# Pairs of row tiles of the second product between the gates and ups of the last columns of the first, in a two-layer encoder

## The chip, the cores and the metric

The kernel runs on one core of a Trainium2 chip. The metric is the device time of one execution in microseconds (us); several runs were timed, and their median counts. The engines have these names: PE (TensorE, matmuls), DVE (VectorE), ACT (ScalarE), POOL (GpSimd), SP (SyncE, which issues the loads).

## The reference

Two layers over x of 256 tokens by 1024, float32. Each layer has an FFN, a mixer of two attention groups, and an FFN, with a LayerNorm behind each. The change touches the four FFNs alone. D_FF is 2816.

```python
def swiglu(x, w_in, w_out):
    h = x @ w_in
    gate, up = h[..., :D_FF], h[..., D_FF:]
    return (jax.nn.silu(gate) * up) @ w_out
...
for l in range(DEPTH):
    x = layer_norm(ALPHA * x + 0.5 * swiglu(x, ffn1_w_in[l], ffn1_w_out[l]), ln_g[l, 0], ln_b[l, 0])
    mix = hybrid_mixer(x, cos, sin, mask, w_in[l], w_out[l], diff_lambda[l],
                       diff_subln_g[l], swa_sink[l], lambda_init)
    x = layer_norm(ALPHA * x + mix, ln_g[l, 1], ln_b[l, 1])
    x = layer_norm(ALPHA * x + 0.5 * swiglu(x, ffn2_w_in[l], ffn2_w_out[l]), ln_g[l, 2], ln_b[l, 2])
```

## The kernel before

**Halves.** Every float32 operand is split in two parts, a high one (wh, gh) and the low rest (wl, gl), and a product is the sum of three matmuls: wh with gh, wl with gh, wh with gl. A row of weights (128 x 1024) comes by a DMA of 512 KB into `raw`; ACT casts it to wh (L118), DVE subtracts to get wl (L119). `Weights.get` makes rows ahead of their use, up to LOOK + 1 = 9 tiles of wh and wl; a pair (below) counts as four. Five `raw` buffers take the loads, and a pair uses three of them.

**One FFN** (named by layer and number: 00, 02, 10, 12) is made of these stages, in this order on PE, whose order is the order of the code. The other engines' instructions are set into order by a scheduler with priorities; the making of weights (`LATER`) comes behind other work that is ready.

- `first`: column tiles 0 to 3 of the first product (of 22, JT), from 8 rows of weights, and their transposes.
- `col` for columns 4 and 5 alone, then for two columns at once: (6, 7) to (20, 21). A column has a gate half and an up half, each with one PSUM bank: 8 wide matmuls (wh against both parts of x, 512 columns, L419) and 8 narrow ones (wl against the high part, 256 columns, L424). Two columns take four of the eight PSUM banks; the next two take the other four. Once a half is done, ACT copies its narrow part out (L434), and DVE adds the two parts (L435), which frees the bank. Then come silu, the product (L438) and the split into g (L441, L442).
- The second product. Its 22 row tiles belong to the columns of the same number. A single (`step`) multiplies one row tile for both token tiles and both halves of the width: 12 matmuls of 512 columns. Two row tiles together can be a pair (`pair`), after Strassen and Winograd: seven products in place of eight, 21 matmuls for 24. For this DVE makes four sums of the weights (L86 to L89) and the split of all of them, and `sums` makes four sums of g (L457 to L462). Pairs are those of columns (6, 7) to (16, 17), STR = 3 to 8. `PLAN` sets singles and pairs behind one another: three singles, six pairs. Four banks (acc) take the output, four more (pp: products 5, 7, 1, 6) what the outputs have in common.
- Behind the last pair the pp are added into x on DVE (L541 to L550), and a tail of TAIL = 7 singles goes over token tile 0, then over token tile 1, so that the LayerNorm of tile 0 runs beside the matmuls of tile 1. The transposes for the next stage follow.

Of the kernel before, what the change touches and what calls it, by code (L numbers as in the profile page):

```python
# [19 lines left out]
P = 128  # L20
# [13 lines left out]
TAIL = 7  # L34
SPLIT = 3
TCUT = 3
LOOK = 8
# [3 lines left out]
STR = (3, 4, 5, 6, 7, 8)  # L41
PLAN = "o o S o S S S S S"
# [17 lines left out]
class Weights:  # L60
# [6 lines left out]
    def _halves(self, i, raw, nm=""):  # L67
        nc = self.nc
        n = raw.shape[-1]
        wh = self.pool.tile([P, 1024], F32R, tag="wh", name=f"wh{i}{nm}", bufs=9)  # L70
        wl = self.pool.tile([P, 1024], F32R, tag="wl", name=f"wl{i}{nm}", bufs=9)
        nc.scalar.copy(wh[:, 0:n], raw)
        nc.vector.tensor_tensor(wl[:, 0:n], raw, wh[:, 0:n].bitcast(F32), ALU.subtract)
        return [tuple(w[:, c : c + 512] for w in (wh, wl)) for c in range(0, n, 512)]
# [21 lines left out]
    def _slots(self, i):  # L96
        return 4 if self.srcs[i][0] == "S" else 1

    def _make(self, i):
        nc = self.nc  # L100
        if self.srcs[i][0] == "S":
            return self._make_pair(i)
        raw = self.pool.tile([P, 1024], F32, tag="raw", name=f"raw{i}", bufs=5)
        wh = self.pool.tile([P, 1024], F32R, tag="wh", name=f"wh{i}", bufs=9)
        wl = self.pool.tile([P, 1024], F32R, tag="wl", name=f"wl{i}", bufs=9)

        n = 512 if i < 3 else 1024
        src = self.srcs[i]

        rows = src if isinstance(src, tuple) else (src,)  # L110
        for c in range(0, 1024, n):
            s = slice(c, c + n)
            for q, r in enumerate(rows):
                h = P // len(rows)

                (nc.sync if i or c else nc.scalar).dma_start(raw[q * h : (q + 1) * h, s], r[:, s])
            with self.tc.high_priority(0 if i < 3 else -LATER):
                nc.scalar.copy(wh[:, s], raw[:, s])  # L118
                nc.vector.tensor_tensor(wl[:, s], raw[:, s], wh[:, s].bitcast(F32), ALU.subtract)  # L119
        self.made.append((wh, wl))  # L120
# [15 lines left out]
def encoder_kernel(  # L136
# [36 lines left out]

    singles = [k for k in range(JT) if k // 2 not in STR]
    singles, tail = singles[: len(singles) - TAIL], singles[len(singles) - TAIL :]
    plan, left, pairs = [], list(singles), list(STR)
    for u in PLAN.split():
        plan.append((u, (left if u == "o" else pairs).pop(0)))
    assert not left and not pairs

    def out_rows(w):
        row = lambda k: w[k * P : (k + 1) * P, :]
        rows = [row(k) if u == "o" else ("S", row(2 * k), row(2 * k + 1)) for u, k in plan]
        return rows + [row(k) for k in tail]

    srcs = []
    for l in range(DEPTH):
        srcs += [f1_b[l, k] for k in range(KT)]
        srcs += [f1_in[l, j, s] for j in range(JT - NB) for s in range(2)]
        srcs += out_rows(f1_out[l])  # L190
# [8 lines left out]
        srcs += [f2_b[l, k] for k in range(KT)]  # L199
        srcs += [f2_in[l, j, s] for j in range(JT - NB) for s in range(2)]  # L200
        srcs += out_rows(f2_out[l])
# [159 lines left out]
    def ffn(l, n, last=False):  # L361
        nonlocal wi
        nm = f"{l}{n}"
        gs = [gp.tile([P, 2, 2, SEQ], F32R, tag="g", name=f"g_{nm}_{q}") for q in range(JT // 2)]
# [29 lines left out]
        def first_t(gv, t):  # L394
            tr = ps.tile([P, 4, P], F32, tag="b", name=f"trg_{nm}{t}")
            for i in range(4):
                nc.tensor.transpose(tr[:, i, :], gv[:, i * P : (i + 1) * P], ident)
            for q in range(2):
                a = slice(t * P, (t + 1) * P)
                dh = gs[q][:, :, 0, a]  # L400
                nc.scalar.copy(dh, tr[:, 2 * q : 2 * q + 2, :])
                dv.tensor_tensor(gs[q][:, :, 1, a], tr[:, 2 * q : 2 * q + 2, :], dh.bitcast(F32), ALU.subtract)

        def col(*js, flip=False):
# [3 lines left out]
            for j in js:  # L408

                hs = [ps.tile([P, 2, SEQ], F32, tag="b", name=f"h{'gu'[s]}_{nm}_{j}") for s in range(2)]  # L410
                tl = tp.tile([P, 2, SEQ], F32, tag="tl", name=f"tl_{nm}_{j}", bufs=2)
# [3 lines left out]

            def wide(hs, ws, s):
                for k in range(KT):

                    mm(hs[s], ws[s][0][:, k * P : (k + 1) * P], xx[:, k], start=(k == 0 and not flip),  # L419
                       stop=(k == KT - 1 and flip), skip_group_check=flip)  # L420

            def narrow(hs, ws, s):
                for k in range(KT):
                    mm(hs[s][:, 1, :], ws[s][1][:, k * P : (k + 1) * P], xx[:, k, 0], start=(k == 0 and flip),  # L424
                       stop=(k == KT - 1 and not flip), skip_group_check=flip)

            one, two = (narrow, wide) if flip else (wide, narrow)
            for j, hs, tl, ws in ts:
                for s in range(2):
                    one(hs, ws, s)  # L430
            for j, hs, tl, ws in ts:
                for s in range(2):
                    two(hs, ws, s)
                    nc.scalar.copy(tl[:, s], hs[s][:, 1, :])  # L434
                    dv.tensor_tensor(tl[:, s], hs[s][:, 0, :], tl[:, s], ALU.add)  # L435
                nc.scalar.activation(tl[:, 0], tl[:, 0], AF.Silu)  # L436
                gv = tl[:, 1]
                dv.tensor_tensor(gv, tl[:, 0], gv, ALU.mult)  # L438
                q, jj = divmod(j, 2)
                n = P if q in STR and jj == 0 else SEQ  # L440
                nc.scalar.copy(gs[q][:, jj, 0, 0:n], gv[:, 0:n])  # L441
                dv.tensor_tensor(gs[q][:, jj, 1, 0:n], gv[:, 0:n], gs[q][:, jj, 0, 0:n].bitcast(F32), ALU.subtract)  # L442
                if q in STR and jj:
                    sums(q, ts[0][2][:, 1], gv)

        sm = {}
# [31 lines left out]
        for j in (NB + 1, *range(NB + 2, JT, 2)):  # L478

            col(*((j,) if j == NB + 1 else (j, j + 1)), flip=(j % 4 == 0 or j == NB + 1))  # L480
# [8 lines left out]
        k0, k1 = singles[0], tail[-1]  # L489
        kl = tail[-SPLIT]  # L490
        acc = [[(slice(512 * h, 512 * h + 512), ps.tile([P, 512], F32, tag="b", name=f"acc_{nm}_{t}{h}"),
                 k0, tail[-SPLIT - 1] if last and t and h else k1) for h in range(2)] for t in range(2)]
# [12 lines left out]
        pp = {}  # L505

        def pair(q, w, first, final):
            b11, b21, b22, t4, t1, t2, t3 = w
            if first:
                for c in (5, 7, 1, 6):  # L510
                    pp[c] = ps.tile([P, 512], F32, tag="b", name=f"pp_{nm}_{c}")
            sh, sl = sm[q]
            blk = lambda kk, t: [gs[q][:, kk, e, t * P : (t + 1) * P] for e in range(2)]
            smb = lambda c: (sh[:, c], sl[:, c])
            s1, s2, s3, s4 = (smb(c) for c in range(4))
            for o, (ah, al), (bh, bl) in (
                (acc[0][0][1], blk(1, 0), b21),
                (acc[0][1][1], s4, b22),
                (pp[5], s1, t1),
                (pp[7], s3, t3),  # L520
                (pp[1], blk(0, 0), b11),
                (pp[6], s2, t2),
                (acc[1][0][1], blk(1, 1), t4),
            ):
                own = any(o is p for p in pp.values())
                for e, (g, ww) in enumerate(((ah, bh), (ah, bl), (al, bh))):
                    mm(o, g, ww, start=(own and first and e == 0), stop=(own and final and e == 2))  # L527

        for u, k in plan:
            w = W.get(wi)  # L530
            wi += 1
            if u == "S":
                pair(k, w, k == STR[0], k == STR[-1])
            else:
                for t in range(2):
                    step(k, w, t, acc[t])
        v = tp.tile([P, 512], F32, tag="tmp", name=f"v_{nm}")
        c = 0.5 / ALPHA
        lo, hi = slice(0, 512), slice(512, 1024)
# [17 lines left out]
        if last:  # L557

            fin = [acc[1][0]] + [(slice(o, o + 256), ps.tile([P, 256], F32, tag="b", name=f"acc_{nm}_1{o}"),
                                  kl, k1) for o in (512, 768)]  # L560
# [421 lines left out]
```

## Time and profile before

| what | value |
|---|---|
| median of 3 runs | 930.16 us |
| lowest, highest | 928.87, 930.35 us |
| profiled execution, its own time | 929.28 us |
| its span, first to last instruction | 927.5 us |
| mean granted clock of PE | 0.997 |
| DMA, mean over the span | 190 GB/s |

The page of the profile gives busy time and share of the span for each engine. In rows of a group stands the line, the engine, the operation, what it writes and reads (out<-in) with the shapes, the count, the busy time with the mean of one in ns, and the idle time of the engine just before them with what ended it. In rows of the timeline stands the start, the duration, then the same names, and in brackets the idle time ahead, where there was any. A row with x8 is eight instructions in a run. In a view by windows each stretch has a row. Matmuls are pipelined: a row of eight ends later than the next begins, and a matmul's cost is the distance between starts.

### The profile page before, as it was taken

How to read it: one execution, taken by the hardware profiler on the slowest of the kernel's cores; microseconds unless marked ns; L12 is line 12 of the kernel's file. 1: busy time of each engine (PE TensorE's matmuls, PEld its weight loads, DVE VectorE, ACT ScalarE, POOL GpSimd, SP SyncE). 2: the span in 40 equal slices, each digit the busy share in tenths (PEclk: the TensorE clock that was granted, in tenths of full speed). 3: DMA queues.
4: the chain of work that ended last, by engine and by line, in shares of the span. 5: the costliest groups of instructions: out<-in, count | busy, mean ns of one | idle time of the engine just before them, and what ended most of it. 6: DMA issues, size and time to landing. Idle time of an engine off the chain costs nothing.

```text
span 927.5 us, 13795 instructions
## 1 busy us (share of the span) xinstructions
PE 919.1 (99%) x4958; PEld 784.9 (85%) x4958; DVE 804.9 (87%) x1388; ACT 577.8 (62%) x982; POOL 17.0 (2%) x27
## 2 busy tenths in 40 slices
PE   9999999999999999999999999999999999999996
PEld 6888888888878888888888888888888888888885
DVE  7898899998987677899986888999988876888997
ACT  5768656546865666656646666664478656666660
POOL 0000000000000000000000000000000000000000
PEclk9999999999999999999999999999999999999998
DMA  8976445774426755545775665466844365665451
GB/s 320 313 265 203 160 137 191 246 260 154 128 90 206 248 182 182 159 136 191 257 262 196 187 192 168 136 231 208 290 112 137 100 236 188 189 192 163 136 205 46
DMA packets 51380, 176.30 MB, mean 190 GB/s; under 512 B 6512, under 2 KB 8304, under 8 KB 51312
## 3 DMA queue, kind: packets, MB, share of 16 engines
q1 hardware_dynamic: 51024, 175.03, 58.0%
q8 instruction: 39, 0.64, 0.3%
q10 hardware_dynamic: 288, 0.39, 0.1%
q14 instruction: 29, 0.24, 0.1%
HBM read 174.35 MB, written 1.05 MB: 189 GB/s over the span
## 4 chain that ended last, share of the span: by engine, by line
PE 98%; DMA 1%; DVE 1%; SPq 0%; issue 0%; ACT 0%; DVEq 0%
PE hg L419 14%; PE hu L419 14%; PE acc L503 12%; PE hb L381 9%; PE hu L424 7%; PE hg L424 7%; PE pp L527 7%; PE acc L527 5%; PE ao L840 5%; PE os L776 1%; PE pj_sq L617 1%; PE pj_sq L619 1%; PE pj_dv L617 1%; PE pj_sq L618 1%; PE pj_dq L618 1%; PE pj_dv L619 1%
## 5 line engine op out<-in xcount | busy, mean ns | idle before, releaser
L119 DVE TENSOR_TENSOR wl<-raw,wh 128x1024 fp32r<-128x1024 f32 (+1 forms) x271 | 325.2, 1207 | 57.0 <-PE hg L424 20.2
L118 ACT CAST wh<-raw 128x1024 fp32r<-128x1024 f32 (+1 forms) x271 | 282.1, 1046 | 99.7 <-PE acc L503 14.8
L419 PE MATMUL hg<-xx,wh 128*128 128x512 f32 x576 | 143.1, 390 | 0.0
L419 PE MATMUL hu<-xx,wh 128*128 128x512 f32 x576 | 142.3, 389 | 0.0
L419 PEld LDWEIGHTS hu<-xx,wh 128*128 128x128 f32 x576 | 108.1, 188 | 22.5
L419 PEld LDWEIGHTS hg<-xx,wh 128*128 128x128 f32 x576 | 106.6, 188 | 21.2
L503 PE MATMUL acc<-wh,g 128*128 128x512 f32 (+1 forms) x326 | 90.5, 386 | 0.0
L424 PE MATMUL hg<-xx,wl 128*128 128x256 f32 x576 | 81.0, 283 | 0.0
L424 PE MATMUL hu<-xx,wl 128*128 128x256 f32 x576 | 80.9, 283 | 0.0
L424 PEld LDWEIGHTS hg<-xx,wl 128*128 128x128 f32 x576 | 75.4, 191 | 1.6
L424 PEld LDWEIGHTS hu<-xx,wl 128*128 128x128 f32 x576 | 74.3, 192 | 0.0
L503 PEld LDWEIGHTS acc<-wh,g 128*128 128x128 f32 x326 | 60.9, 188 | 12.2
L381 PE MATMUL hb<-wh,xx 128*128 128x512 f32 x256 | 69.5, 391 | 0.4 <-ACT wh L118 0.4
L381 PEld LDWEIGHTS hb<-wh,xx 128*128 128x128 f32 x256 | 47.7, 188 | 11.3 <-ACT wh L118 1.6
L503 PE MATMUL acc<-wl,g 128*128 128x512 f32 (+1 forms) x163 | 51.7, 385 | 0.0
L434 ACT COPY tl<-hg 128x256 f32<-128x256 f32 x72 | 26.7, 371 | 30.9 <-PE hg L419 27.4
L434 ACT COPY tl<-hu 128x256 f32<-128x256 f32 x72 | 26.9, 373 | 19.6 <-PE hu L424 16.8
L381 PE MATMUL hb<-wl,xx 128*128 128x512 f32 x128 | 38.9, 390 | 0.0
L441 ACT CAST g<-tl 128x128 fp32r<-128x128 f32 (+1 forms) x72 | 26.7, 371 | 19.2 <-DVE tl L438 18.2
L840 PE MATMUL ao<-wh,xx 128*128 128x512 f32 x128 | 37.0, 398 | 0.0
L503 PEld LDWEIGHTS acc<-wl,g 128*128 128x128 f32 x163 | 30.6, 188 | 6.1
L436 ACT ACTIVATE tl<-tl 128x256 f32<-128x256 f32 x72 | 30.1, 418 | 6.5 <-DVE tl L435 5.7
(1140 smaller groups left out, 1576.3 us busy)
## 6 DMA issues: line engine op xcount, KB each, us to landing
raw<-in_f_in_dram SPq DMA_DIRECT2D x144, 512.0 KB, 4.4
raw<-in_f_out_dram SPq DMA_DIRECT2D x40, 512.0 KB, 4.5
raw<-in_m_in_dram SPq DMA_DIRECT2D x36, 512.0 KB, 4.4
raw<-in_f_b_dram SPq DMA_DIRECT2D x29, 512.0 KB, 4.3
raw<-in_m_out_dram SPq DMA_DIRECT2D x8, 512.0 KB, 5.0
raw<-in_m_out_dram SPq DMA_DIRECT2D x16, 256.0 KB, 4.4
lng<-in_ln_g_dram SPq DMA_DIRECT2D x6, 512.0 KB, 4.9
lnb<-in_ln_b_dram SPq DMA_DIRECT2D x6, 512.0 KB, 6.2
```

What stands on the lines that cost most here:

```text
L118: nc.scalar.copy(wh[:, s], raw[:, s])
L119: nc.vector.tensor_tensor(wl[:, s], raw[:, s], wh[:, s].bitcast(F32), ALU.subtract)
L381: mm(hb[s], xx[:, k, g, t, :], ww[:, 512 * s : 512 * s + 512], start=(k == 0 and e == 0), stop=(k == KT - 1 and e == 2))
L419: mm(hs[s], ws[s][0][:, k * P : (k + 1) * P], xx[:, k], start=(k == 0 and not flip), stop=(k == KT - 1 and flip), skip_group_check=flip)
L424: mm(hs[s][:, 1, :], ws[s][1][:, k * P : (k + 1) * P], xx[:, k, 0], start=(k == 0 and flip), stop=(k == KT - 1 and not flip), skip_group_c ...
L434: nc.scalar.copy(tl[:, s], hs[s][:, 1, :])
L436: nc.scalar.activation(tl[:, 0], tl[:, 0], AF.Silu)
L441: nc.scalar.copy(gs[q][:, jj, 0, 0:n], gv[:, 0:n])
L503: mm(a, g, ww[:, s], start=(k == ka and e == 0), stop=(k == kb and e == 2))
L527: mm(o, g, ww, start=(own and first and e == 0), stop=(own and final and e == 2))
L617: mm(o, xx[:, k, 0, t, :], wh[:, s], start=(k == 0), stop=False)
L840: mm(acc[t][h], xx[:, k, g, t, :], ww[:, s], start=(k == 0 and e == 0), stop=(k == KT - 1 and e == 2))
```

## The change

- There are seven pairs in each FFN, those of columns (4, 5) to (16, 17), STR = 2 to 8. No single stands ahead of the pairs any more, and the tail has eight.
- The pairs stand among the columns. From column MIX = 14 on, columns come one by one: three products of a pair (9 matmuls), the gate half, the other four products (12 matmuls), the up half. Column 20 has the seventh pair, column 21 none.
- All seven products of the pairs have a bank of their own from column 14 to 20 (pp 1 to 7; products 2, 3 and 4 go on as the acc banks in the tail), so that the gate and up halves of these columns share the one bank that is left. The fourth acc bank is taken after column 21.
- LOOK is 7 for 8: eight tiles of wh and wl of 1024 columns; the halves of 512 columns of a pair have two tiles of their own, and a pair counts as three.
- The high and low parts of the sums of pairs 5 to 8 are in the pool of g, and tiles of g are taken when they are written first.

```diff
-TAIL = 7
+TAIL = 8
-LOOK = 8
+LOOK = 7
-STR = (3, 4, 5, 6, 7, 8)
-PLAN = "o o S o S S S S S"
+STR = (2, 3, 4, 5, 6, 7, 8)
+MIX = 14
...
     def _halves(self, i, raw, nm=""):
...
-        wh = self.pool.tile([P, 1024], F32R, tag="wh", name=f"wh{i}{nm}", bufs=9)
-        wl = self.pool.tile([P, 1024], F32R, tag="wl", name=f"wl{i}{nm}", bufs=9)
+        tag, bufs = ("", LOOK + 1) if n == 1024 else ("f", 2)
+        wh = self.pool.tile([P, n], F32R, tag="wh" + tag, name=f"wh{i}{nm}", bufs=bufs)
+        wl = self.pool.tile([P, n], F32R, tag="wl" + tag, name=f"wl{i}{nm}", bufs=bufs)
...
-        return 4 if self.srcs[i][0] == "S" else 1
+        return 3 if self.srcs[i][0] == "S" else 1
...
+        def half(j, s, tl):
+            nonlocal wi
+            h, w = bank(j, s), W.get(wi)
+            wi += 1
+            wide(h, w)
+            narrow(h, w)
+            gather(h, tl, s)
...
-            if STR.index(q) < 3:
-                s = xp.tile([P, 2, 4, P], F32R, tag="x", name=f"s_{nm}_{q}")
-                sh, sl = s[:, 0], s[:, 1]
-            else:
-                sh, sl = (tp.tile([P, 4, P], F32R, tag="tmp", name=f"s{c}_{nm}_{q}") for c in "hl")
+            pool, tag = (xp, "x") if STR.index(q) < 3 else (gp, "g")
+            s = pool.tile([P, 2, 4, P], F32R, tag=tag, name=f"s_{nm}_{q}")
+            sh, sl = s[:, 0], s[:, 1]
...
-        for j in (NB + 1, *range(NB + 2, JT, 2)):
+        for j in (NB + 1, *range(NB + 2, MIX, 2)):
...
+        def pair(i, w):
+
+            b11, b21, b22, t4, t1, t2, t3 = w
+            q = STR[i]
...
+            todo = ((2, blk(1, 0), b21), (3, s4, b22), (5, s1, t1), (7, s3, t3),
+                    (1, blk(0, 0), b11), (6, s2, t2), (4, blk(1, 1), t4))
+            for m, (c, (ah, al), (bh, bl)) in enumerate(todo):
+                if c not in pp:
+                    pp[c] = ps.tile([P, 512], F32, tag="b", name=f"pp_{nm}_{c}")
+                if m == 3:
+                    yield
+                for e, (g, ww) in enumerate(((ah, bh), (ah, bl), (al, bh))):
+                    mm(pp[c], g, ww, start=(i == 0 and e == 0), stop=(c in (1, 5, 6, 7) and i == len(STR) - 1 and e == 2))
+            yield
+
+        for j in range(MIX, JT):
+            tl = tl_tile(j)
+            if j - MIX < len(STR):
+                w = W.get(wi)
+                wi += 1
+                run = pair(j - MIX, w)
+            for s in range(2):
+                if j - MIX < len(STR):
+                    next(run)
+                half(j, s, tl)
+            gated(j, tl)
+            loads(j)
+
...
+        c22 = ps.tile([P, 512], F32, tag="b", name=f"acc_{nm}_11")
+        acc = [[(lo, pp[2], None, tail[-1]), (hi, pp[3], None, tail[-1])],
+               [(lo, pp[4], None, tail[-1]), (hi, c22, tail[0], tail[-SPLIT - 1] if last else tail[-1])]]
```

`gather` is the copy and the add (L434, L435 before; L418, L419 after), `gated` is silu, product and split, both as they were.

The order of PE at column 14 of FFN 00, before: the wide matmuls of columns 14 and 15 in four banks (hg and hu are gate and up, xx is the transposed x), then the narrow ones.

```order
L419 MATMUL hg_00_14_999<-xx_78,wh28_766 128x512 x8
L419 MATMUL hu_00_14_1000<-xx_78,wh29_772 128x512 x8
L419 MATMUL hg_00_15_1014<-xx_78,wh30_781 128x512 x8
L419 MATMUL hu_00_15_1015<-xx_78,wh31_787 128x512 x8
L424 MATMUL hg_00_14_999<-xx_78,wl28_767 128x256 x8
L424 MATMUL hu_00_14_1000<-xx_78,wl29_773 128x256 x8
L424 MATMUL hg_00_15_1014<-xx_78,wl30_782 128x256 x8
L424 MATMUL hu_00_15_1015<-xx_78,wl31_788 128x256 x8
```

The same place now, from the last matmuls of a pair's first three products (pp is a product, s a sum of g) to the second group:

```order
L531 MATMUL pp_00_5_1027<-wl28t_785,s_00_2_470 128x512
L531 MATMUL pp_00_5_1027<-wh28t_784,s_00_2_470 128x512
L409 MATMUL hg_00_14_1032<-xx_78,wh29_889 128x512 x8
L414 MATMUL hg_00_14_1032<-xx_78,wl29_890 128x256 x8
L531 MATMUL pp_00_7_1031<-wh28t_784,s_00_2_470 128x512
L531 MATMUL pp_00_7_1031<-wl28t_785,s_00_2_470 128x512
```

Each half now stands alone, wide and narrow together, with a part of a pair on each side; nine matmuls of products 1, 6 and 4 and then the up half follow.

The order of DVE in FFN 02, now, behind the add of the up half of column 17: the making of a pair's weights (raw128, wl128, t4), the gating of column 17 (L424, L430), the sums of g for pair 8 (sf, s; L476 to L481), and in the last row the add of the gate half of column 18.

```order
L89 TENSOR_TENSOR raw128a_4356<-raw128b_4357,raw128t_4358 128x512
L424 TENSOR_TENSOR tl_02_17_4245<-tl_02_17_4245 128x256
L74 TENSOR_TENSOR wl128b_4367<-raw128b_4357,wh128b_4366 128x1024
L476 TENSOR_TENSOR sf_02_8_4347<-tl_02_16_4138,tl_02_17_4245 128x128
L430 TENSOR_TENSOR g_02_8_4238<-tl_02_17_4245,g_02_8_4238 128x256
L477 TENSOR_TENSOR sf_02_8_4347<-tl_02_16_4138,sf_02_8_4347 128x128
L90 TENSOR_TENSOR t4_128_4361<-raw128b_4357,raw128a_4356 128x512
L479 TENSOR_TENSOR sf_02_8_4347<-tl_02_17_4245,sf_02_8_4347 128x128
L74 TENSOR_TENSOR wl128t_4371<-raw128t_4358,wh128t_4370 128x1024
L74 TENSOR_TENSOR wl128a_4375<-raw128a_4356,wh128a_4374 128x1024
L481 TENSOR_TENSOR s_02_8_4348<-sf_02_8_4347,s_02_8_4348 128x512
L419 TENSOR_TENSOR tl_02_18_4355<-hg_02_18_4391,tl_02_18_4355 128x256
```

Before, most of the making of pairs' weights stood behind the adds of all columns; now it stands between them.

The order of DVE in FFN 00, now, at the last columns: from the add of gate 20 over rows of weights to the adds of the products 1, 6 and 5 (L566 to L571) and the add of up 20 among them.

```order
L419 TENSOR_TENSOR tl_00_20_1652<-hg_00_20_1668,tl_00_20_1652 128x256
L120 TENSOR_TENSOR wl51_1655<-raw51_1653,wh51_1654 128x1024
L120 TENSOR_TENSOR wl52_1671<-raw52_1669,wh52_1670 128x1024
L566 SCALAR_TENSOR_TENSOR x_in0_596<-pp_00_1_1066,x_in0_596 128x512
L569 TENSOR_TENSOR v_00_1803<-pp_00_6_1070,v_00_1803 128x512
L120 TENSOR_TENSOR wl53_1677<-raw53_1675,wh53_1676 128x1024
L419 TENSOR_TENSOR tl_00_20_1652<-hu_00_20_1717,tl_00_20_1652 128x256
L571 TENSOR_TENSOR u_00_1807<-pp_00_5_1027,v_00_1803 128x512
```

The adds of the products stood behind all columns and pairs (L541 to L550); they now start before the columns end.

More of the change, by code (lines that the diff above doesn't have):

```diff
@@ L171, in encoder_kernel, with ffn_rows @@
     dv = nc.vector
[L174 to L183, printed above, removed]
+    tail = [k for k in range(JT) if k // 2 not in STR]
+    assert len(tail) == TAIL and len(STR) <= JT - MIX
+    def ffn_rows(b, w_in, w_out):
+        row = lambda k: w_out[k * P : (k + 1) * P, :]
+        rows = [b[k] for k in range(KT)]
+        for j in range(NB, JT):
+            if j >= MIX and j - MIX < len(STR):
+                q = STR[j - MIX]
+                rows.append(("S", row(2 * q), row(2 * q + 1)))
+            rows += [w_in[j - NB, 0], w_in[j - NB, 1]]
         return rows + [row(k) for k in tail]
@@ L408, in col @@
             for j in js:
-                hs = [ps.tile([P, 2, SEQ], F32, tag="b", name=f"h{'gu'[s]}_{nm}_{j}") for s in range(2)]
-                tl = tp.tile([P, 2, SEQ], F32, tag="tl", name=f"tl_{nm}_{j}", bufs=2)
+                hs = [bank(j, s) for s in range(2)]
+                tl = tl_tile(j)
                 ws = [W.get(wi), W.get(wi + 1)]
@@ L414, in col @@
                 ts.append((j, hs, tl, ws))
[L416 to L425, printed above, removed]
             one, two = (narrow, wide) if flip else (wide, narrow)
@@ L477, in ffn, with loads @@
         first_t(g1, 1)
[L478 to L480 removed]
+        def loads(j):
+            nonlocal gb
             if first_x and j == NB + 2:
```

113 lines of the change are left out of this document (53 added, 60 removed).

## The prediction, made before the changed kernel had run

> **What bounds the kernel now.** I read the page first: busy times, the granted clock in slices, and the chain that ended last.
>
> ```profile
> PE 919.1 (99%) x4958; PEld 784.9 (85%) x4958; DVE 804.9 (87%) x1388; ACT 577.8 (62%) x982; POOL 17.0 (2%) x27
> PEclk9999999999999999999999999999999999999998
> PE 98%; DMA 1%; DVE 1%; SPq 0%; issue 0%; ACT 0%; DVEq 0%
> ```
>
> TensorE (PE) works for 99% of the span at nearly the full clock, and it is 98% of the chain. A matmul less is a matmul of time less, as long as nothing else makes PE wait. VectorE (DVE) at 87% is the engine to watch. So I cut one FFN (layer 0, second: "02") at its stages: columns 4 to 13, columns 14 to 21, the singles and pairs, the last seven rows.
>
> ```profile
> core 0: us, PE busy (x) PEld busy (x) DVE busy (x) ACT busy (x) POOL busy (x), PEclk, DMA share, GB/s
> 305.80:361.90 56.10, 56.10 (x328) 49.75 (x327) 41.92 (x78) 35.95 (x66) 0.00 (x0) 1.00 0.63 197
> 361.90:406.30 44.40, 44.40 (x258) 39.37 (x256) 38.48 (x73) 28.71 (x52) 0.00 (x0) 1.00 0.51 156
> 406.30:443.00 36.70, 36.70 (x163) 30.41 (x162) 35.44 (x43) 23.04 (x27) 0.00 (x0) 1.00 0.56 186
> 443.00:462.80 19.80, 19.80 (x93) 16.46 (x92) 19.80 (x29) 11.57 (x13) 0.92 (x1) 1.00 0.71 245
> ```
>
> PE is full in every stage. VectorE's load is uneven: 87% in columns 14 to 21, 97% in the pairs. It never stops PE there, because columns have four PSUM banks and their results wait, and because halves of the weights are made rows ahead. The change moves pairs among columns and takes three of the four banks away. That is where the time is decided.
>
> **What goes: twelve matmuls.** Two row tiles as singles are 24 matmuls of 512 columns (3 products, 2 token tiles, 2 halves of the width, twice); as a pair they are 21. Each FFN makes a seventh pair, so 3 matmuls go per FFN, 12 in all.
>
> ```profile
> 133.52 0.39 PE L527 MATMUL acc<-wh46b,g 128*128 128x512 f32 x1
> ...
> 138.28 0.61 PE L503 MATMUL acc<-wh,g 128*128 128x512 f32 x2
> ```
>
> Between these lie the 21 matmuls of one pair: 4.76 us, 0.227 each (the duration of 0.39 is latency; start to start counts). 12 x 0.227 = **2.72 us** saved at most: 929.28 - 2.72 = 926.56. The profiled execution (929.28) lies 0.88 below the median of the runs shown, 930.16, and within their spread; I keep to it.
>
> **What PE does in the mixed stretch.** A half column (gate or up) is 8 wide and 8 narrow matmuls.
>
> ```profile
> 394.22 1.12 PE L424 MATMUL hu<-xx,wl 128*128 128x256 f32 x8
> 395.18 1.12 PE L424 MATMUL hg<-xx,wl 128*128 128x256 f32 x8
> ...
> 400.86 1.98 PE L419 MATMUL hu<-xx,wh 128*128 128x512 f32 x8
> 402.67 1.98 PE L419 MATMUL hg<-xx,wh 128*128 128x512 f32 x8
> ```
>
> 0.96 + 1.81 = 2.77 us. The order of the mixed stretch is 9 matmuls of a pair (2.04), gate (2.77), 12 matmuls (2.72), up (2.77): a unit of 10.3 us. No instruction is dearer there than in the stretches it came from.
>
> **The wait that is added.** All halves of columns 14 to 20 use one bank. A half may start once the half before it has been gathered: ScalarE copies the narrow part, VectorE adds (L434, L435; L418, L419 after). Up's start is covered by 12 matmuls behind the gate (2.72 us), the next gate's by 9 (2.04). PE is in order: what waits at the head of a half holds the pair's matmuls behind it too, and ready ones among them cannot pass. So the **lag** counts, from a half's last matmul to the end of its add.
>
> ```profile
> 315.66 0.84 PE L419 MATMUL hu<-xx,wh 128*128 128x512 f32 x3
> ...
> 316.26 0.42 DVE L435 TENSOR_TENSOR tl<-hg,tl 128x256 f32<-128x256 f32 x1 [1.19 <-ACT tl L434]
> 395.94 0.41 DVE L435 TENSOR_TENSOR tl<-hg,tl 128x256 f32<-128x256 f32 x1
> 396.27 0.41 DVE L435 TENSOR_TENSOR tl<-hu,tl 128x256 f32<-128x256 f32 x1
> ```
>
> With VectorE idle (it waited 1.19) the lag is 316.68 - 315.66 = 1.02 (the gate ended where up began). With a full queue, the gate of column 19, which ended where the up at 394.22 began, was added by 395.94 + 0.41 = 396.35: 2.13. In the middle, 1.58. All lie under 2.72, and 2.13 just misses 2.04: in the mean the bank is covered, and what costs is where VectorE has much to do ahead of an add.
>
> **What VectorE must do per stretch.** I price its instructions start to start in a full queue.
>
> ```profile
> 137.43 0.69 DVE L86 TENSOR_TENSOR raw50t<-raw50a 128x512 f32<-128x512 f32 x1
> ...
> 144.10 1.22 DVE L73 TENSOR_TENSOR wl50t<-raw50t,wh50t 128x1024 fp32r<-128x1024 f32 x1
> 145.24 1.22 DVE L73 TENSOR_TENSOR wl50a<-raw50a,wh50a 128x1024 fp32r<-128x1024 f32 x1
> ...
> 148.18 1.22 DVE L73 TENSOR_TENSOR wl51b<-raw51b,wh51b 128x1024 fp32r<-128x1024 f32 x1
> 149.31 0.68 DVE L88 TENSOR_TENSOR raw51a<-raw51b,raw51t 128x512 f32<-128x512 f32 x1
> 149.91 1.22 DVE L73 TENSOR_TENSOR wl51t<-raw51t,wh51t 128x1024 fp32r<-128x1024 f32 x1
> ...
> 159.87 1.23 DVE L119 TENSOR_TENSOR wl<-raw,wh 128x1024 fp32r<-128x1024 f32 x1
> ...
> 388.17 0.28 DVE L457 TENSOR_TENSOR sf<-tl,tl 128x128 f32<-128x128 f32 x1
> 388.37 0.68 DVE L87 TENSOR_TENSOR raw132t<-raw132a,raw132b 128x512 f32<-128x512 f32 x1
> ```
>
> 1024 elements: 1.135 (1.14 and 1.13); 512: 0.60; 256: 0.33 (the two adds above); 128: 0.20. Together they fall a little short: from 137.43 to 159.87 stand 11 of 1024 and 16 of 512, by these 22.09, measured 22.44, 1.6% more.
>
> In the changed order, from the add of gate 14 to that of gate 20 in FFN 02, VectorE has 30 instructions of 1024, 29 of 512, 22 of 256 and 10 of 128: 34.05 + 17.4 + 7.26 + 2.0 = 60.7, with the 1.6% 61.7. PE has six units, 61.8. **The two are level**: a burst is caught up only slowly. The worst burst is the piece of VectorE's order shown with the change (FFN 02; 10 and 12 have the same): behind the add of up 17, twelve instructions up to the add of gate 18, three of 1024, three of 512, three of 256, three of 128: 3.405 + 1.8 + 0.99 + 0.6 = 6.80, with 1.6% 6.90. PE needs 2.04 + 2.77 = 4.81 from one half's end to the other's. The lag grows by 2.09: from 1.58 to 3.67, and the cover is 2.72. Up 18 starts **0.95 us late**. Then the queue is short (five instructions to the next add, against 5.49 of PE), and the next long piece (to gate 19: 6.22, with 1.6% 6.32, against 4.81) ends at a lag of 1.02 + 1.51 = 2.53, still covered by 2.72. Worked through in this way, FFN 00, whose order differs, loses 0.15 once.
>
> So 3 x 0.95 + 0.15 = 3.0. From below: with the lag of 1.02 ahead of the burst 3 x 0.39 = 1.2. From above, with 2.13: 3 x 1.5 + 0.15 = 4.6. I take the middle. To it comes ScalarE, which stands ahead of each add with its copy.
>
> ```profile
> L118 ACT CAST wh<-raw 128x1024 fp32r<-128x1024 f32 x265 | 278.3, 1056 | 94.6 <-PE acc L503 14.8 <-PE hg L419 11.9 <-PE hu L419 10.1
> 402.87 0.37 ACT L434 COPY tl<-hu 128x256 f32<-128x256 f32 x1 [0.20 <-PE hu L419]
> ```
>
> Here the copy met an idle engine. But a cast of 1.06 us is under way in 278.3/927.5 = 30% of the time, and met in its middle it delays the copy by 0.53: 0.16 a copy. Six halves are near their limit (gates 18 and 19 in three FFNs): 1.0 us; bounds 0 and 6 x 1.06 = 6.4. Stalls in all: **4.0 us**.
>
> **What else moves, at nothing.** The halves of a pair's weights are made among the columns rather than in a block; the instructions are the same but for one more pair per FFN, 44 more on VectorE in the whole program, all priced above or hidden under a full PE in the tail. The look-ahead is one row shorter (eight tiles for nine); between pairs PE takes 2.77 us a row, and a load lands in 4.4 to 4.5:
>
> ```profile
> raw<-in_f_in_dram SPq DMA_DIRECT2D x144, 512.0 KB, 4.4
> raw<-in_f_out_dram SPq DMA_DIRECT2D x40, 512.0 KB, 4.5
> ```
>
> A unit loads four rows of 0.52 MB, 2.1 MB in 10.3 us, 204 GB/s; the last stage above moved 245 beside a full PE, so SyncE's queue keeps up. If it doesn't, the price is a late cast, which is the ScalarE term. The tail has 8 rows for 7: 12 matmuls moved, none new, and they give the LayerNorm 1.36 us more cover. Column 21 has no pair ahead of it, but its gate and up take the banks of products 1 and 6, not the shared one: on VectorE's order the adds from those banks (L566, L569) stand ahead of the add of up 20, some 5 us before they are needed.
>
> **The sum:** 929.28 - 2.72 + 4.0 = **930.6 us**.
>
> **The rivals.**
>
> (a) *All adds come in time.* Speaks for it: VectorE's sum is just under PE's, and lags of 1.02 were seen. Against: the burst of 6.9 against 4.81 needs a lag under 0.63 ahead of it. No stall: 929.28 - 2.72 = **926.6**.
>
> (b) *VectorE becomes the bound of the mixed stretch: slower.* Its place is columns 14 to 20, its price each microsecond over PE's 61.8 in an FFN, and it decides from 2% over my prices (60.7 x 1.02 = 61.9). At 5% over, 63.7 against 61.8, 1.9 an FFN and the bursts beside it: row by row 2.7 in 02, 10 and 12, 1.6 in 00, 9.6 in all, **936.2**. For it: 1.6% of the 2 is in the trace already, and every wait of VectorE on a cast counts. Against: where VectorE was at 97%, it did not slip.
>
> (c) *Column 21 does wait for the one bank*, or the banks of 1 and 6 come as late as that: two adds without cover in each FFN, 8 x 1.02 = 8.2 and no other stall: 926.56 + 8.16 = **934.7**. Against it speaks the order of VectorE.
>
> (d) *The clock drops in the mixed stretch*, because PE now stops and starts there.
>
> ```profile
> 0.77 3.92 PE L217 MATMUL wps<-const-bfloat16-1.0 128*128 128x512 bf16 x9 [0.77 <-PEq L971]
> ```
>
> After idling, nine matmuls of 512 columns took 3.92 us, 0.436 each, against 0.227: 1.9 us lost. Once per FFN 7.5: 930.6 + 7.5 = **938.1**. Against: the granted clock was 1.00 in all four stages above, and my stops are about 1 us, an idling far shorter than a start from nothing. The Trainium skill, "TensorE: Matmul & The Clock Gate", section "A second HAM failure mode: psum-queue depth-cycling", tells of a kernel in which PSUM banks cycled and PE paused so often that the clock swung between half and full; the same page puts the idle gap that loses the clock at some 3 us. By the first the time would be that of (d), by the second that of the forecast, and no row of before shows pauses of this kind.
>
> **How the numbers follow.** About 0.2% (1.86 us) is what a measurement of this kernel can tell from no change: faster means stalls under 0.86, slower over 4.6. Chances: forecast 0.56, with a range of its own from 1.2 to 5.6 of stalls (4.6 and the 1.0), 927.8 to 932.2; (a) 0.17; (b) 0.19; (c) 0.04; (d) 0.04. Of the forecast's 0.56 I put 0.04 below and 0.07 above the band. Faster: 0.17 + 0.04 = 0.21. Slower: 0.19 + 0.04 + 0.04 + 0.07 = 0.34. Same: 0.45. The range runs from (a), 926.5, to (b) at 5%, 936.2; outside it lie (d), (b) beyond 5%, and half of (a)'s scatter, together under 0.2.
>
> **What the profile after would show.** Right: PE's matmul count 12 lower; idle time on PE ahead of L409 hu of column 18 in FFNs 02, 10 and 12, near 1 us, released by VectorE's add in L419, and little elsewhere; VectorE near 98% busy from column 14 to 20; no idle time at column 21; clock 1.00. Idle time at most halves of columns 14 to 20 would speak for (b), at column 21 for (c), a clock under 0.95 for (d). The forecast is wrong if PE waits on casts of weights or loads at the head of a pair (the look-ahead too short), or if idle time stands where I count none: at the banks of column 14 or ahead of the tail.

## The result and the profile after

| | median | runs |
|---|---|---|
| before | 929.88 us | 4, 928.87 to 930.35 |
| changed | 936.1 us | 4, 934.96 to 938.29 |
| ratio | 1.0071 | 95% interval 1.0051 to 1.0092 |

The changed kernel is slower by 0.7%, 6.2 us. The profiled execution took 935.84 us with a span of 933.4, 5.9 more than before. Its page has these lines on the engines, the clock and the chain:

```profile
PE 919.9 (99%) x4946; PEld 781.4 (84%) x4946; DVE 821.1 (88%) x1432; ACT 571.3 (61%) x991; POOL 17.0 (2%) x27
PEclk9999999999999999999999999999999999999999
PE 31%; DVE 3%; DMA 1%; ACT 1%; issue 1%; DVEq 0%; ACTq 0%; SPq 0%
```

The twelve matmuls are gone (4946 for 4958) and the clock is full. But the chain no longer runs on PE from end to end: steps on VectorE, ScalarE and loads stand in it. The same stages of FFN 02 as before, by windows; first columns 4 to 13, then the mixed stretch, columns 14 to 20:

```profile
core 0: us, PE busy (x) PEld busy (x) DVE busy (x) ACT busy (x) POOL busy (x), PEclk, DMA share, GB/s
306.60:362.70 56.10, 56.10 (x327) 49.78 (x326) 46.94 (x90) 36.57 (x68) 0.00 (x0) 1.00 0.53 177
362.70:437.00 74.30, 72.33 (x367) 61.16 (x366) 71.61 (x108) 49.65 (x74) 0.00 (x0) 1.00 0.65 206
```

In the mixed stretch PE lacks 2.0 us, VectorE is busy for 96%, and the loads run at 206 GB/s, for 156 in columns 14 to 21 before. The view of PE's waits names what it waits for, with the total, the times and the longest:

```profile
PE hu L409 <- DVE tl L419: 3.2, 5, 1.0
PE hg L409 <- DVE tl L419: 2.4, 3, 1.2
```

All eight waits stand at the head of a half in the mixed stretch, and all end with VectorE's add, as foreseen. This view counts from a matmul's modelled end. Taken from start to start of the matmuls, over the usual 0.227, the eight add to 6.9 us (0.60 and 0.92 in FFN 00, 0.98 and 1.31 in 02, 1.17 and 0.39 in 10, 1.16 and 0.33 in 12). The first matmul behind each wait takes 0.11 more.

One of the eight is the burst that the prediction worked out. From VectorE's timeline, the add of up 17 and what stands behind it; the second row of PE's is the half that waits:

```profile
405.33 0.42 DVE L419 TENSOR_TENSOR tl<-hu,tl 128x256 f32<-128x256 f32 x1 [0.21 <-ACT tl L418]
405.68 0.68 DVE L89 TENSOR_TENSOR raw128a<-raw128b,raw128t 128x512 f32<-128x512 f32 x1
...
411.56 0.69 DVE L481 TENSOR_TENSOR s<-sf,s 128x512 fp32r<-128x512 f32 x1
412.17 0.42 DVE L419 TENSOR_TENSOR tl<-hg,tl 128x256 f32<-128x256 f32 x1
```

```profile
411.44 0.39 PE L531 MATMUL pp<-wh125f,g 128*128 128x512 f32 x1
412.64 1.20 PE L409 MATMUL hu<-xx,wh 128*128 128x512 f32 x4 [0.81 <-DVE tl L419]
```

From add to add 6.84 us (6.90 forecast); up 18 starts 412.64 - 411.44 - 0.227 = 0.97 late (0.95 forecast). The same half waits in FFNs 10 and 12.

Other waits begin elsewhere. In FFN 00, ahead of gate 15, a row of VectorE's making of the pair before, then the rows of SyncE, ScalarE, VectorE and PE:

```profile
88.69 1.22 DVE L74 TENSOR_TENSOR wl31t<-raw31t,wh31t 128x1024 fp32r<-128x1024 f32 x1
```

```profile
89.97 0.33 SPq L83 DMA_DIRECT2D raw34b<-in_f_out_dram  x1
```

```profile
94.64 1.05 ACT L73 CAST wh34b<-raw34b 128x1024 fp32r<-128x1024 f32 x1 [3.35 <-DMA raw34b<-in_f_out_dram]
95.60 0.36 ACT L418 COPY tl<-hu 128x256 f32<-128x256 f32 x1
```

```profile
95.99 0.42 DVE L419 TENSOR_TENSOR tl<-hu,tl 128x256 f32<-128x256 f32 x1 [0.55 <-ACT tl L418]
```

```profile
96.47 1.20 PE L409 MATMUL hg<-xx,wh 128*128 128x512 f32 x4 [0.44 <-DVE tl L419]
```

Up 14 was done at 93.80, where the next pair's matmuls begin. Its copy is due then, but ahead of it in ScalarE's order stands the cast of a pair's second row, and that row, issued at 89.97, has not landed. It was issued right behind VectorE's last reading of raw31t, a buffer of the pair before (88.69 + 1.22 = 89.91). ScalarE is idle for 3.35 us, the last 0.84 of them with the copy ready behind the cast, and then the cast itself takes its time. Copy, add and the next half come late one after the other: up 14's copy starts 1.80 after its matmuls, where 0.20 was seen before. The Trainium skill, "TensorE: Matmul & The Clock Gate", section "Architectural detail: the array is 16× 32×32, not 1× 128×128", calls ScalarE and VectorE strict first-in-first-out queues; these rows agree.

A late load stands ahead of the other seven waits too, in most of them less directly. Ahead of the burst at up 18 in FFN 02 it holds the copy of up 17, with whose add the burst begins:

```profile
403.98 1.05 ACT L73 CAST wh128b<-raw128b 128x1024 fp32r<-128x1024 f32 x1 [3.38 <-DMA raw128b<-in_f_out_dram]
404.94 0.36 ACT L418 COPY tl<-hu 128x256 f32<-128x256 f32 x1
```

So the burst begins with a lag of 1.7 us in FFN 02 and, by the like rows, of 1.9 in FFNs 10 and 12, where 1.58 was forecast. Ahead of up 19 in FFNs 10 and 12 the copy of up 18 is held in the same way, by a cast that is idle for 2.4. Ahead of gate 19 in FFN 00 VectorE is idle for 0.88 until ScalarE has cast a tile of g, which stood behind a pair's cast idle for 2.02. At gate 20 in FFN 02, the longest wait, the copy of up 19 stands behind the cast of a single row:

```profile
427.44 1.05 ACT L119 CAST wh<-raw 128x1024 fp32r<-128x1024 f32 x1 [2.60 <-PE pp L531]
```

The view puts this idle time down to PE, but the row's load was issued at 421.69 and landed at 427.36, just before the cast began.

Twenty casts of pairs wait for their load in this kernel, 41.9 us in all; in the kernel before it is one, for 0.4. The longest of them before and after, and what SyncE waits for most ahead of a pair's loads (the last sum of the pair before, which frees a buffer), by the views of the waits:

```profile
ACT wh46b L72 <- DMA raw46b<-in_f_out_dram: 0.4, 1, 0.4
```

```profile
ACT wh46b L73 <- DMA raw46b<-in_f_out_dram: 3.8, 1, 3.8
```

```profile
SPq L83 <- DVE t L90: 61.5, 15, 6.3
```

### The profile page after: what moved, and what is told of

It is laid out like the page before. It is cut to its first block, busy times and chain, and to the rows that moved or that the text cites. A ratio compares the mean times of both kernels' runs of the same rounds, so it can differ in the third digit from the quotient of the medians.

```text
span 933.4 us, 13768 instructions
## 1 busy us (share of the span) xinstructions
PE 919.9 (99%) x4946; PEld 781.4 (84%) x4946; DVE 821.1 (88%) x1432; ACT 571.3 (61%) x991; POOL 17.0 (2%) x27
## 5 line engine op out<-in xcount | busy, mean ns | idle before, releaser
L119 ACT CAST wh<-raw 128x1024 fp32r<-128x1024 f32 (+1 forms) x263 | 273.4, 1045 | 111.3 <-PE acc L562 26.9
L120 DVE TENSOR_TENSOR wl<-raw,wh 128x1024 fp32r<-128x1024 f32 (+1 forms) x263 | 314.4, 1205 | 28.6 <-ACT wh L119 12.4
L414 PEld LDWEIGHTS hu<-xx,wl 128*128 128x128 f32 x576 | 76.2, 191 | 2.5
L562 PE MATMUL pp<-wh,g 128*128 128x512 f32 x192 | 57.9, 389 | 0.0
L562 PEld LDWEIGHTS pp<-wh,g 128*128 128x128 f32 x192 | 35.8, 188 | 7.2
L418 ACT COPY tl<-hu 128x256 f32<-128x256 f32 x72 | 26.6, 370 | 20.9 <-PE hu L414 18.7
L419 DVE TENSOR_TENSOR tl<-hu,tl 128x256 f32<-128x256 f32 x72 | 29.9, 416 | 7.1 <-ACT tl L418 6.9
L429 ACT CAST g<-tl 128x128 fp32r<-128x128 f32 (+1 forms) x72 | 26.1, 362 | 15.6 <-DVE tl L424 14.8
L418 ACT COPY tl<-hg 128x256 f32<-128x256 f32 x72 | 26.4, 366 | 13.7 <-PE hg L409 12.4
L419 DVE TENSOR_TENSOR tl<-hg,tl 128x256 f32<-128x256 f32 x72 | 29.9, 415 | 4.1 <-ACT tl L418 4.0
```

Source lines behind the costliest of these rows:

```text
L414: mm(h[:, 1, :], w[1][:, k * P : (k + 1) * P], xx[:, k, 0], start=(k == 0 and flip), stop=(k == KT - 1 and not flip), skip_group_check=flip)
L418: nc.scalar.copy(tl[:, s], h[:, 1, :])
L419: dv.tensor_tensor(tl[:, s], h[:, 0, :], tl[:, s], ALU.add)
L562: mm(a, g, ww[:, s], start=(k == ka and e == 0), stop=(k == kb and e == 2))
```

## The experiments

Two theories stood after the result. **Theory Q**: VectorE's program order, the making of weights in bursts ahead of an add. **Theory S**, later named L: a pair holds three of the five buffers for loaded rows, so rows are loaded late, ScalarE's casts wait, and a half's copy waits behind them.

### e1_pool_sums: the four sums of a pair on GpSimd

```diff
-            dv.tensor_tensor(ta[:, a], r0[:, b], r0[:, a], ALU.subtract)
+            nc.gpsimd.tensor_tensor(ta[:, a], r0[:, b], r0[:, a], ALU.subtract)
```

and the other three likewise.

> The four sums of a pair's weight rows (four instructions of 512 elements, 0.60 us each on VectorE) are made on GpSimd instead, nothing else. Theory Q (VectorE's program order: the making of a pair's weights stands in a burst ahead of a half's add, and the half waits for it): 2.4 us less on VectorE for each 10.3 us of PE, so the bursts fit under the cover; the stalls of that kind (hu of column 18 in three FFNs 3.6, gate 20 in FFN 00 1.0, up 14 in FFN 00 0.2: 4.9 of 8.0 us) go: 936.1 - 4.9 = about 931, and with nothing else left 928. Theory S (ScalarE's program order: a cast that waits for a pair's load or for a free weight tile holds the copy of a half behind it): about 3.1 us of stalls stay, near 931, or more if GpSimd keeps the loaded rows longer than VectorE did. GpSimd has no such row in any trace so far: if its four sums take over 10.3 us, the casts of a pair come late and PE waits ahead of pairs: slower than 936.

Measured: 1010.85 us against 929.6, ratio 1.089 (1.0858 to 1.0923). VectorE slows down beside GpSimd:

```profile
391.98 1.21 DVE L120 TENSOR_TENSOR wl<-raw,wh 128x1024 fp32r<-128x1024 f32 x1
...
393.97 2.30 DVE L120 TENSOR_TENSOR wl<-raw,wh 128x1024 fp32r<-128x1024 f32 x1
```

```profile
393.93 1.26 POOL L87 TENSOR_TENSOR raw119t<-raw119a 128x512 f32<-128x512 f32 x1 [8.43 <-DMA raw119a<-in_f_out_dram]
```

```profile
396.87 3.78 PE L409 MATMUL hu<-xx,wh 128*128 128x512 f32 x8 [4.95 <-DVE tl L419]
```

The same instruction takes 1.21 alone and 2.30 with GpSimd at work beside it. What is taken from VectorE's queue comes back in the duration of the rest: with 112 instructions fewer VectorE is busy for 869.3 us, for 821.1 in the changed kernel. The expectation had a slower time for another reason, four sums of over 10.3 us; those of this pair take 1.26 + 1.60 + 1.61 + 2.14 = 6.6. The run says nothing on Q against S; it shows how fast the time rises once adds are late, and the last row shows a second loss: after 4.95 us of waiting the eight wide matmuls take 3.57 us to the next row where 1.81 is normal. The granted clock, by windows of this kernel:

```profile
397.00:400.00 3.00, 3.00 (x7) 2.37 (x8) 3.00 (x3) 2.43 (x4) 2.92 (x2) 0.50 0.55 186
```

### e2_raw6 and its control e5_work5: a sixth buffer for loaded rows

```diff
-        r0, r1, ta = (self.pool.tile([P, 1024], F32, tag="raw", name=f"raw{i}{c}", bufs=5) for c in "abt")
+        r0, r1, ta = (self.pool.tile([P, 1024], F32, tag="raw", name=f"raw{i}{c}", bufs=6) for c in "abt")
-        raw = self.pool.tile([P, 1024], F32, tag="raw", name=f"raw{i}", bufs=5)
+        raw = self.pool.tile([P, 1024], F32, tag="raw", name=f"raw{i}", bufs=6)
-    tp = ctx.enter_context(tc.tile_pool(name="tp", bufs=7))
+    tp = ctx.enter_context(tc.tile_pool(name="tp", bufs=5))
```

> A sixth buffer for loaded rows (two work tiles of 512 elements fewer to make room). Theory S: a pair's second row is loaded late because its buffer is free late; with a sixth the cast is not held, the stalls of gate 15 in FFN 00 (0.7) and up 19 in FFNs 10 and 12 (0.9) go: about 934.5; gate 20 of FFN 02 (1.4, a cast that waits for a weight tile) stays. Theory Q: VectorE's order is the same, so nothing changes: 936, and hu 18 in FFNs 02, 10 and 12 keeps its 1.1 to 1.3 in both.

Measured: 931.68 us, ratio 1.0018 (1.0009 to 1.0027): 4.4 us of the 6.2 are gone, more than expected. The same row of weights as above is now there:

```profile
92.06 1.05 ACT L73 CAST wh34b<-raw34b 128x1024 fp32r<-128x1024 f32 x1 [0.71 <-DMA raw34b<-in_f_out_dram]
94.05 0.37 ACT L418 COPY tl<-hu 128x256 f32<-128x256 f32 x1 [0.94 <-PE hu L414]
```

The row was issued at 88.7, 1.3 earlier, and landed in 3.3 us for 4.6; the copy waits for its matmuls and for nothing else. The waits at gate 15 in FFN 00 and at up 19 are gone, and so are two that I had put down to other causes (gate 19 in FFN 00, which the expectation of e1_pool_sums calls gate 20, and gate 20 in FFN 02). One of 0.30 at gate 15 in FFN 02 is new. Up 18 in FFNs 02, 10 and 12 keeps 0.67 each: theory Q's part. The copy of up 17 comes 0.20 behind its matmuls there, and the burst begins with a lag of 1.4.

The control takes the last line of the edit alone.

> Control for the sixth buffer of e2_raw6: only the work tiles go from seven to five, the buffers for loaded rows stay five. Theory L (a pair holds three of the five buffers, so rows are loaded late and ScalarE's casts wait for them with a half's copy behind): no change against the changed kernel, 936. Rival: the fewer work tiles moved something in the order of the engines, and that was the gain: about 931.7, as e2_raw6.

Measured: 935.8 us, ratio 1.0067 (1.0053 to 1.0081), the changed kernel's time. The gain of e2_raw6 is the buffer's.

### e6_raw4: four buffers

The edit is that of e2_raw6 with 4 in place of 6, and the work tiles left at seven.

> Four buffers for loaded rows for five, nothing else. Theory L: a pair then leaves one buffer for the next rows, casts come later still: well above 938, the step from five to four at least as large as that from six to five (4.4 us), so 940 or more. Rival (only VectorE's order counts): the sum of that order, row by row, gives 4.5 us of stalls for 3.3: about 937.

Measured: 953.63 us, ratio 1.0253 (1.0239 to 1.0267). PE's waits:

```profile
PE hu L409 <- DVE tl L419: 15.2, 15, 2.4
PE hg L409 <- DVE tl L419: 3.4, 5, 1.4
```

Six, five, four buffers: 931.7, 936.1, 953.6. The order of VectorE's work alone would have given 1.2 more by the expectation's sum; theory L holds, and the step grows. The casts of pairs don't wait longer in all than with five buffers (38.7 us for 41.9); those of single rows do, 90.1 for 22.6.

### e3_late_split: VectorE's order alone

```diff
-            nc.scalar.copy(sh, f)
-            dv.tensor_tensor(sl, f, sh.bitcast(F32), ALU.subtract)
             sm[q] = sh, sl
+
+            def split():
+                nc.scalar.copy(sh, f)
+                dv.tensor_tensor(sl, f, sh.bitcast(F32), ALU.subtract)
+
+            if q == STR[-1]:
+                late.append(split)
+            else:
+                split()
...
             gated(j, tl)
+            if j == MIX + 4:
+                late.pop()()
```

> The cast and the low part of the sums of the last pair (columns 16, 17) are made after column 18 instead of after 17. In VectorE's order two instructions (512 and 1024 elements) now stand behind the add of gate 18 and not ahead of it: 5.06 us ahead of it for 6.80. Theory Q: hu 18 in FFNs 02, 10 and 12 no longer waits (3.6 us less), some of it comes back at gate 19 and up 19 (0.5 an FFN by the same sum): about 934. Theory S, for all of the loss: no change, 936.

Measured: 933.63 us, ratio 1.004 (1.0025 to 1.0055), as theory Q said. Up 18 doesn't wait any more in FFNs 02, 10 and 12; some 0.2 to 0.6 appears at later halves. So **both** theories hold a part: 4.4 us by the buffer, 2.5 by the order, each alone.

### e8_fix: both repairs

The edits of e2_raw6 and e3_late_split, and `LATER = 300`.

> Three repairs together: the sixth buffer for loaded rows (work tiles five), the late split of the last pair's sums (e3_late_split), and the making of weights put 300 instead of 100 places behind in priority. Theories L and Q together: late loads go (4.4 us less, as in e2_raw6), hu 18 no longer waits (2.0 of the 2.4 left there), 1.6 us stay by VectorE's order (up 19, 0.5 in three FFNs), 1.2 us by the slower matmuls behind narrow ones: 929.6 - 2.7 + 1.6 + 1.2 = about 929.7, the same as before the change. If the repairs hinder each other: 931.7 or more. Only if the slower matmuls were no loss of their own could it come under 928.5.

Measured: 930.06 us, ratio 1.0003 (0.9994 to 1.0012): the time of before, and near what the sum gave, 929.7. `LATER = 300` was not tried alone.

### e9_swap_loads: the two loads of a pair in the other order

```diff
-        for r, src in zip((r0, r1), self.srcs[i][1:]):
+        for r, src in zip((r1, r0), self.srcs[i][:0:-1]):
             nc.sync.dma_start(r, src)
```

> The changed kernel with the two loads of a pair in the other order (second row first), nothing else; five buffers. ScalarE's first cast of a pair reads the second row, so it no longer waits for the later load; VectorE's first sum reads the first row and now does. Theory L by ScalarE (the late row holds the copy behind the cast): the stalls that begin at such a cast (gate 15 in FFN 00, up 19 in FFNs 10 and 12: 1.6 us) go, and VectorE's order, which moves too, sums to 0.7 us of stalls for 3.3: about 932. If VectorE is held by the later load in the same way, half or more comes back: 934 to 936.

Measured: 929.62 us, ratio 0.9997 (0.9987 to 1.0007). That is 2.4 less than the 932 expected: without any more memory the swap brings back as much as both repairs:

```profile
92.42 1.05 ACT L73 CAST wh34b<-raw34b 128x1024 fp32r<-128x1024 f32 x1 [0.59 <-DMA raw34b<-in_f_out_dram]
94.55 0.37 ACT L418 COPY tl<-hu 128x256 f32<-128x256 f32 x1 [1.08 <-PE hu L414]
```

```profile
PE hg L409 <- DVE tl L419: 0.5, 1, 0.5
```

Fourteen casts of pairs wait for their load, 9.5 us in all (20 and 41.9 in the changed kernel), and VectorE's waits for loads of pairs, which the rival foresaw, are two of 0.3. The one wait is that of the view; from start to start three halves are late, 1.2 us in all. VectorE's order moved as well, so the run gives no split of its gain between the two; e2_raw6 and e3_late_split split the loss of the changed kernel, not this gain.

### e10_fix_swap: all three

The edits of e8_fix and of e9_swap_loads.

> e8_fix with the two loads of a pair swapped. With six buffers rows are hardly late any more, and the sum over VectorE's order is the same 1.6 us: no change against e8_fix within 0.1%, about 930 and the same as before the change. Under 929 only if rows were still late in e8_fix on ScalarE.

Measured: 930.18 us, ratio 1.0007 (0.9998 to 1.0016), no change against e8_fix. Ten casts of pairs still wait for their load in e8_fix, 9.4 us in all, and none here; the time doesn't hang on them.

### e11_swap_late: no wait left

```diff
-LATER = 100
+LATER = 500
```

on top of e9_swap_loads.

> e9_swap_loads with the making of weights 500 instead of 100 places behind in priority. By the sum over VectorE's order no half waits any more (0.7 us in e9_swap_loads, there measured as 1.3). What is left is then the 2.7 us of matmuls less and the slower matmuls behind narrow ones: 56 more changes from narrow to 512 columns, 0.026 us each, 1.5 us. Expected 929.6 - 2.7 + 1.5 = 928.4, faster than before by 0.1%. If the slower matmuls were not a loss of their own: 927. If stalls come back elsewhere: 929.6, as e9_swap_loads, or more.

Measured: 928.35 us against 929.16 us, ratio 0.999 (0.9981 to 0.9999). One wait is left:

```profile
PE hg L409 <- DVE tl L419: 0.4, 1, 0.4
```

This is faster than both kernels, though by 0.1% only: of the 2.7 us of twelve matmuls 0.8 stay. What takes most of the other 1.9 is not a wait. In the changed kernel's timeline, the matmuls of a pair behind a half:

```profile
420.37 0.40 PE L531 MATMUL pp<-wh128t,s 128*128 128x512 f32 x1
420.60 0.40 PE L531 MATMUL pp<-wl128t,s 128*128 128x512 f32 x1
420.84 0.39 PE L531 MATMUL pp<-wh128t,s 128*128 128x512 f32 x1
421.07 0.40 PE L531 MATMUL pp<-wh128a,g 128*128 128x512 f32 x1
421.30 0.39 PE L531 MATMUL pp<-wl128a,g 128*128 128x512 f32 x1
421.53 0.39 PE L531 MATMUL pp<-wh128a,g 128*128 128x512 f32 x1
```

Five steps take 1.16 us for 5 x 0.227 = 1.13: a change from narrow matmuls to those of 512 columns costs 0.026. In the mean over all changes the extra is the same 0.026 to 0.027, and there are 76 for 20 before: 56 x 0.026 = 1.5 us. The other side of a change gives some of it back: the first narrow matmul behind wide ones comes after 0.113 us, the next ones after 0.120. That leaves 0.02 a change, 1.1 us.

### e7_look7: the shorter look-ahead in the kernel before

```diff
-LOOK = 8
+LOOK = 7
...
-        return 4 if self.srcs[i][0] == "S" else 1
+        return 3 if self.srcs[i][0] == "S" else 1
```

with the halves' tiles as in the change, and nothing else of it.

> The kernel before the change with only the look-ahead of the change: eight tiles of 1024 columns for nine, two of 512 for a pair's last half, a pair counted as three. If the shorter look-ahead costs nothing by itself: 929.6, no change. If a part of the loss came from it: up to 6 us more. PE waited for no weights in the changed kernel, so I expect no change within 0.1%.

Measured: 934.68 us, ratio 1.0052 (1.0036 to 1.0067), a miss. The waits are at places where the changed kernel has none:

```profile
PE tr_y L328 <- DVE x L356: 1.4, 3, 1.0
PE pj_dk L619 <- DVE wl L120: 1.3, 2, 0.7
```

The transposes behind the LayerNorm and the mixer's weights come late; from start to start these waits are 4.4 us more than before. In the changed kernel, which has the same look-ahead, both are in time. It has one row more in the tail and other work ahead of it; which of these hides the wait was not tried.

### e4_pairs_behind: seven pairs behind the columns

```diff
-MIX = 14
+PLAN = "S o S S S S S S"
```

with the loops of before, a sixth x tile for sums, and one tile of 512 for a pair's last half.

> Seven pairs, but behind all columns as before the change (one single after the first pair, a tail of seven; columns two at a time with four banks). Same 12 matmuls fewer. If the loss is only in the shared bank, it goes whole: 929.9 - 2.7 = about 927.2. Rival: VectorE needs 7 x 6.42 = 44.9 us for the pairs' weights against 36.0 us of PE in that stage; what is not made ahead (up to 9 us in each FFN) becomes a wait of PE for weights: up to 960.

Measured: 947.14 us, ratio 1.0182 (1.0167 to 1.0198). The rival came true. In each FFN PE waits for the weights of a pair:

```profile
PE pp L535 <- DVE wl51f L74: 2.4, 1, 2.4
```

This is the half with only one tile in this kernel, so the run shows that seven pairs in a row outrun their weights here, and not how much of it is VectorE's rate and how much the tile. The same wait stands in all four FFNs. By windows behind it, in FFN 10 and in FFN 12 (the number before the last two is the granted clock):

```profile
633.90:636.30 2.40, 2.40 (x11) 1.96 (x12) 2.40 (x4) 1.96 (x3) 0.00 (x0) 1.00 0.94 357
916.80:919.20 2.40, 2.40 (x6) 1.92 (x7) 2.40 (x4) 1.66 (x3) 0.00 (x0) 0.50 0.97 394
```

Of four waits of 2.4 us one cost the clock.

## Why the prediction went wrong

The forecast was 930.6, no change; the time was 936.1, slower, near the upper end of the range. By its steps:

- **Twelve matmuls, 2.7 us less**: right. The count is 4946, and e11_swap_late shows what is left of the gain once the waits are gone.
- **The wait at the shared bank, and its place**: right. Every wait of PE in the mixed stretch is a half's, released by VectorE's add.
- **The burst at up 18, 0.95 in FFNs 02, 10 and 12**: right in its place and in the length of the burst, 6.84 for 6.90; the sizes are 0.98, 1.17 and 1.16, and e3_late_split took them away by moving two instructions. That the size fits so well is in part luck: the lag ahead of the burst was put at 1.58 as a middle value, and it was 1.7 to 1.9 because a late load held up 17's copy. With that out of the way, in e2_raw6, the burst costs 0.67, between the lower bound of 0.39 and the 0.95.
- **ScalarE's term, 1.0 us**: here it failed. I took it for casts in progress, 0.16 a copy, and put the late loads beside it at nothing: "SyncE's queue keeps up", from a rate of 204 GB/s against 245 seen. The rate was there (206 in the mixed stretch). But a queue that moves enough bytes can still issue late: what limits it is when a buffer comes free, and a pair holds three of five until VectorE has made its weights. A cast then stands idle at the head of ScalarE's queue, for up to 3.8 us and not for the half of a cast, and what stands behind it comes late: a half's copy, or the work that VectorE needs to go on. One more buffer was worth 4.4 us, where the term was 1.0. The bound of 6.4 covered it, but I took a value near its lower end without a row that showed how long rows had to land once pairs stand among columns.
- **"No instruction is dearer there"**: wrong by 1.1 us, 0.02 net for each of 56 more changes between narrow and wide. A stall also costs more than its length: the first matmul behind each of the eight waits took 0.11 more, 0.9 us that the sum put at nothing.
- **Column 21 at nothing, the clock at 1.00**: right, no wait there and a granted clock of 0.998. The waits of 0.3 to 1.3 here cost no clock, and that of 4.95 in e1_pool_sums did (0.50). The Trainium skill, "TensorE: Matmul & The Clock Gate", section "Why this matters for your kernels", puts the idle gap that loses the clock at some 3 us. The runs put it lower and less sharply: one of four waits of 2.4 us in e4_pairs_behind and one of 2.42 in e6_raw4 brought 0.50, while one of 3.26 in e1_pool_sums, ahead of the gate half at 950.77, was followed by 1.00.
- **The look-ahead at nothing**: no wait of the kind that e7_look7 shows stands in the changed kernel, but it doesn't hold as a rule: alone the shorter look-ahead costs 5 us. The changed kernel with the longer one was not run.
- **Rival (b)**, VectorE as the bound at 936.2: the time was met, the mechanism only in part. VectorE was busy for 96% of the mixed stretch, not late throughout; in e9_swap_loads it is busy for 97% there, and the time is that of before.

The sum as measured: -2.7, +6.9 for eight waits, +0.9 for the slow first matmul behind each, +1.1 for the changes of form, -0.7 outside the columns (0.4 from the first matmul to the first gate of FFN 00, 0.3 at its LayerNorm, both shorter than before; the first differs from run to run, 26.1 us here, 26.5 before, 26.9 in e3_late_split): 5.5 of the 5.9 us of span. What is left, 0.4, has no name.

## What to carry to other kernels

Where a bank or buffer is handed from one piece of work to the next, follow the whole chain that frees it through each engine's program order: a ready copy behind a cast that waits for its load is as late as the load. A transfer is in time by its issue, not by its rate: ask which buffer its issue waits for, and how long the longest holder keeps it. Before buying a buffer, look at which of two loads the first instruction in the queue needs; here swapping the two loads, which moved VectorE's order as well, was worth as much as a sixth buffer and a repair of VectorE's order together.

## What the runs showed of the hardware

GpSimd's sums of 512 elements took 1.3 to 2.4 us in e1_pool_sums, and VectorE's instruction of 1024 elements went from 1.21 to 2.30 beside it; ScalarE's casts stayed at 1.04. The Trainium skill, "SBUF — State Buffer", section "SBUF: two separate sides", has VectorE and GpSimd take turns on a shared pair of ports when a VectorE instruction reads two inputs from there: these rows agree.

The granted clock fell to 0.50 behind waits of PE from 2.4 us up, not behind each of them, and behind none of 1.3 or less.

The first 512-column matmuls behind a run of narrow ones came at 0.232 us for 0.227, four or five of them in each of 76 places. Before, there were 20 such places, 0.5 us in all.
